# A hybrid decoder step on one core: B by token through VectorE and DRAM, state products in pairs, dt's sums in one visit

## The chip, the cores and the metric

The program runs on one of the eight NeuronCores of a Trainium2 chip. The metric is the device time of one execution in microseconds. The kernel before takes 1775.49 us in the median of three runs (1774.15 to 1775.97). The execution that was profiled took 1774.69 us, and its profile spans 1773.0 us.

The engines are called TensorE (PE in the profile; its weight loads PEld), VectorE (DVE), ScalarE (ACT), GpSimd (POOL) and SyncE (SP). SP computes nothing; it issues most DMA transfers. A line number L12 is a line of the kernel before.

## The reference, cut to what matters

The step takes 256 new tokens of one prompt and 8 sequences of 8 sample tokens, 320 tokens in all, through one layer. One input projection gives the columns of a gated MLP (u and v) and of a state-space mixer (z, x, B, C, dt). Both results go through an output projection; then a convolutional feed-forward network follows. All is in float32.

The change lies in the state-space mixer. Its state-space part is, cut down:

```python
dt = softplus(dt_raw + dt_bias);  a = -exp(a_log)
da_cs = cumsum(dt * a)                             # within a chunk of 128 tokens
decay = exp(mask(da_cs[t] - da_cs[s]))
cb = einsum("bctgn,bcsgn->bctsg", cc, bc)          # C times B, over the state
y_diag = einsum("bctsgr,bcsgrp->bctgrp", cb * decay, x * dt)
decay_states = exp(da_cs[last] - da_cs)
states = einsum("bcsgn,bcsgr,bcsgrp->bcgrpn", bc, decay_states, x * dt)
y_off = einsum("bctgn,bcgrpn,bctgr->bctgrp", cc, states_in, exp(da_cs))
```

There are 32 heads of 64 in 4 groups; each group has its own B and C with a state of 128. The prompt has two chunks of 128 tokens and starts from a zero state. The sample sequences are one short chunk each and start from given states (8 sequences x 4 groups x 128 x 512 numbers), which are also updated and returned.

## The kernel before, in words

**Tokens and features.** Activations are kept with features on the partitions and the 320 tokens along the row. Each weight product is split in three: weights and activations are each a rounded float32r part and a remainder (hi and lo), and `accumulate` (L153 to L155) multiplies hi by hi, hi by lo and lo by hi. A weight slab of 512 KB is loaded by SP, rounded by ScalarE (`whi`, L124), and its remainder is formed by VectorE (`wlo`, L125). Three slabs are in the buffers at a time. One slab is 8 blocks, so 24 products of TensorE.

**Order of work.** `project` runs an input projection over slabs. `chunk_out` adds four feature blocks of a finished part into the output projection. All other work is written as generators in the list `bg`. `tick` advances the first of them by one step; `project` and `chunk_out` call it after each slab, `rate` times. In `project` the last `quiet` of the 16 feature blocks have no ticks. `finish` advances until a given generator is done. The framework's planner then lays out a fixed order for each engine from priorities and its own model of times; work under `first()` or a high priority is drawn forward, so an operation can stand elsewhere than where it was written. On the chip each engine takes its own order strictly.

**The gate stage.** B and C are projected by `conv_proj` into `bT` and `cT` (features by tokens), then x of group 0. `steps` makes dt. It projects dt to tokens (L500), takes the softplus on VectorE, and after five empty steps goes to TensorE on three ticks: `cs_ps` (L532, L534) for the running sums by token, `csT_ps` (L547, L548) for the same sums by head, stored to DRAM as `dacs_d` and `tot_d`, and `dec_ps` (L560 to L567) for the decays to the end of a chunk; for the last one GpSimd makes a mask, `later_s`, just ahead of the products. Then `gate_mix` works out the MLP's gates by group (`sg`, L752).

**The state-space stage.** When the gate stage's buffers (pool `gp`) are free, pool `sd` takes their room. B is needed by tokens: 16 transposes by TensorE (`by_token` L414, into `bt_ps`), eight of them on rows of sample tokens that `fourfold` has copied four times, since four partition quarters of 32 rows need the same 32 tokens. ScalarE copies the results to `btok` and `bsp` (L802, L805), and VectorE forms remainders in two quarters of `bsp` (L807).

`ssd(g)` is a generator for each group. Its eight sample states are handled as four pairs. For a pair, `with_c` (L908) multiplies the states by C into `yo_ps` in eight TensorE instructions that each use 32 of the 128 columns of the array; `picked` (L913) makes the pair's B, `shrunk` (L919) decays the state on GpSimd, `grown` (L925, L927) multiplies B by x into `up_ps` and adds it to the state, and `store_state` writes it out. `begin` is with_c, picked and shrunk; `end` is grown and the store. Three pairs of state buffers are there, so pair 3 is loaded into those of pair 0 after its store. `x_of_samples` makes `xsp`, the samples' x that `grown` reads. Then `decays` and `products` make y (`y_ps`, L1004).

The groups' tasks run beside `heads_in_next` (x of the next group), `chunk_out` and `heads_out` (z, the norm, and the last product).

The loop of the pairs is:

```python
for i in range(4):
    if i < 3:
        begin(i)
    else:
        sts.append(load_state(3))
    if i:
        end(i - 1)
    yield
    if i == 0:
        x_of_samples(1)
    yield
begin(3)
yo_to_xdt()
```

Of the kernel before, what the change touches and what calls it, by code (L numbers as in the profile page):

```python
# [13 lines left out]
ALU = mybir.AluOpType  # L14
# [20 lines left out]
def hybrid_step(  # L35
# [325 lines left out]
    tot_d = dr.tile([NH, NB], F32, name="tot_d")  # L361
    ssq_d = [dr.tile([P, NT // 32], F32, name=f"ssq_d{i}") for i in range(4)]
# [52 lines left out]

    def fourfold(out, x, i):

        act.copy(out.rearrange("p k (q t) -> p k q t", q=4), x[:, :, NP + 32 * i:NP + 32 * i + 32].unsqueeze(2).to_broadcast([P, 4, 4, 32]))
        return out

    with ExitStack() as mctx:
# [6 lines left out]
        def conv_proj(c0, k0, out, *room):  # L428
# [27 lines left out]
            project(w_in, c0, evac, quiet=6)  # L456

        def heads_in(g, *room):
            xs = op.tile([P, 4, NT], F32, tag="xs", name="xs", bufs=2)
            conv_proj(X0 + 512 * g, 4 * g, lambda j: xs[:, j, :], *room)  # L460
# [27 lines left out]
        def steps():  # L488
# [26 lines left out]
            for n in (13, 11, 9, 7, 5, 3, 1):  # L515
# [9 lines left out]
                                     op0=ALU.mult, op1=ALU.mult)  # L525
            for _ in range(5):
                yield

            pool.memset(sums[:, 2], -3e38)
            ps = misc("cs_ps")  # L530
            for c in range(2):
                pe.matmul(ps[:, NH * c:NH * c + NH], upper, da[:, c], start=True, stop=True)  # L532
            for r in range(2):
                pe.matmul(ps[64 * r:64 * r + 64, 2 * NH:3 * NH], upper_s[:NS], da[:NS, 2], start=True, stop=True, tile_position=(0, 64 * r))  # L534
            dve.tensor_copy(sums[:, 0:2].rearrange("p c h -> p (c h)"), ps[:, :2 * NH])
# [9 lines left out]
            ps = misc("csT_ps")  # L545
            for c in range(2):
                pe.matmul(ps[:NH, P * c:P * c + P], da[:, c], upper, start=True, stop=True)  # L547
            pe.matmul(ps[:NH, NP:NT], da[:NS, 2], upper_s[:NS], start=True, stop=True)  # L548
            dacsT = op.tile([P, NT + NS + 2 * P], F32, tag="dtf", name="dacsT", bufs=1)[:, :NT + NS]
            dve.tensor_copy(dacsT[:NH, NS:], ps[:NH, :NT])  # L550
            dve.tensor_copy(dacsT[:NH, :NS], ps[:NH, NP:NT])
            sp.dma_start(dacs_d, dacsT[:NH])
            totc = op.tile([NH, NB], F32, name="totc")
            dve.tensor_copy(totc, dacsT[:NH, :NS].rearrange("p (b t) -> p b t", b=NB)[:, :, TS - 1])
            sp.dma_start(tot_d, totc)
            yield

            ps = misc("dec_ps")
# [877 lines left out]
```

## Time and profile before

| what | value |
|---|---|
| median of three runs | 1775.49 us (1774.15 to 1775.97) |
| the profiled execution | 1774.69 us, span 1773.0 us |
| TensorE busy | 1765.1 us (100%) |
| VectorE busy | 1173.7 us (66%) |
| ScalarE busy | 817.9 us (46%) |
| GpSimd busy | 274.5 us (15%) |
| mean granted clock | 0.999 |
| moved | 273.17 MB read, 14.84 MB written, 162 GB/s |

The profile is one execution. Its page gives busy time by engine, the span in 40 slices, the DMA queues, the chain of work that ended last, and the costliest groups of instructions. A busy TensorE isn't a TensorE at its best: its products are pipelined, and a product that started late still counts as busy. So the starts of its products, in the chain and in the timeline, say more than its share.

In the chain of waits a row gives start, length, engine, what was written, the line, and how many instructions are taken together. In a list of groups a row ends with the busy time, the mean length in ns, and the idle time of the engine ahead of it. A group with one line can be cut by tile.

### The profile page before, as it was taken

What the parts mean: (1) busy time and instruction counts of PE and PEld (TensorE: products, weight loads), DVE (VectorE), ACT (ScalarE), POOL (GpSimd) and SP (SyncE); (2) the same over time, 40 slices, a digit from 0 to 9 for tenths busy, and PEclk for the clock granted to TensorE, in tenths of its full rate; (3) what the DMA queues carried; (4) which work ended last, traced back from release to release, by engine and by line L of the source; (5) the groups of instructions that cost most, each with busy time, mean ns of one, the idle gap of its engine ahead of it and who ended that gap; (6) DMA issues with size and microseconds to landing.
All of it is one profiled execution on the core that took longest, in us unless ns stands there. A gap on an engine that the chain in (4) does not pass through costs nothing.

```text
span 1773.0 us, 30633 instructions
## 1 busy us (share of the span) xinstructions
PE 1765.1 (100%) x11897; PEld 1711.9 (97%) x11897; DVE 1173.7 (66%) x2015; ACT 817.9 (46%) x1193; POOL 274.5 (15%) x602
## 2 busy tenths in 40 slices
PE   9999999999999999999999999999999999999998
PEld 7789999999999998999999999999999999999998
DVE  7549764657978778678865465656657575656575
ACT  5434555334564556445645334343434343333445
POOL 1202200000331313103211011010102010101004
PEclk9999999999999999999999999999999999999999
DMA  7556645455666666555554554555455544454542
GB/s 261 161 150 171 189 141 159 153 152 182 223 189 195 186 203 188 147 179 158 171 158 147 154 153 148 155 148 153 150 151 158 144 156 145 156 155 145 155 151 102
DMA packets 217297, 290.01 MB, mean 164 GB/s; under 512 B 19264, under 2 KB 146624, under 8 KB 216960
## 3 DMA queue, kind: packets, MB, share of 16 engines
q1 hardware_dynamic: 205424, 268.84, 50.1%
q10 hardware_dynamic: 10016, 14.16, 2.2%
q0 software_dynamic: 1712, 5.05, 1.0%
q8 instruction: 94, 1.54, 0.4%
q14 instruction: 51, 0.42, 0.1%
HBM read 273.17 MB, written 14.84 MB: 162 GB/s over the span
## 4 chain that ended last, share of the span: by engine, by line
PE 98%; DVE 1%; issue 0%; ACT 0%; ACTq 0%; DVEq 0%
PE ps L153 19%; PE ps L154 19%; PE ps L155 19%; PE pd L153 10%; PE pd L155 10%; PE pd L154 10%; PE ps_v L144 7%; PE y_ps L1004 1%; PE up_ps L925 0%; PE sg L752 0%; PE yo_ps L908 0%; PE xt_ps L414 0%; PE early L70 0%; PE x1p L1299 0%; DVE xsp L863 0%
## 5 line engine op out<-in xcount | busy, mean ns | idle before, releaser
L125 DVE TENSOR_TENSOR wlo<-wraw,whi 128x1024 fp32r<-128x1024 f32 (+1 forms) x476 | 582.3, 1223 | 421.4 <-ACT whi L124 419.6
L124 ACT CAST whi<-wraw 128x1024 fp32r<-128x1024 f32 (+1 forms) x475 | 495.1, 1042 | 714.5 <-PE ps L154 381.5
L153 PE MATMUL ps<-h_hi,whi 128*128 128x320 f32 x2268 | 700.6, 309 | 0.0
L154 PE MATMUL ps<-h_lo,whi 128*128 128x320 f32 x2268 | 699.3, 308 | 0.0
L155 PE MATMUL ps<-h_hi,wlo 128*128 128x320 f32 x2268 | 698.9, 309 | 0.0
L153 PEld LDWEIGHTS ps<-h_hi,whi 128*128 128x128 f32 x2268 | 425.7, 188 | 2.5 <-issue 1.6
L154 PEld LDWEIGHTS ps<-h_lo,whi 128*128 128x128 f32 x2268 | 425.8, 188 | 0.7
L155 PEld LDWEIGHTS ps<-h_hi,wlo 128*128 128x128 f32 x2268 | 425.6, 188 | 0.0
L155 PE MATMUL pd<-fhi,wlo 128*128 128x320 f32 x704 | 217.0, 308 | 0.0
L153 PE MATMUL pd<-fhi,whi 128*128 128x320 f32 x704 | 217.0, 308 | 0.0
L154 PE MATMUL pd<-flo,whi 128*128 128x320 f32 x704 | 217.0, 308 | 0.0
L153 PE MATMUL pd<-ohi,whi 128*128 128x320 f32 x448 | 139.1, 310 | 0.0
L155 PE MATMUL pd<-ohi,wlo 128*128 128x320 f32 x448 | 138.4, 309 | 0.0
L154 PE MATMUL pd<-olo,whi 128*128 128x320 f32 x448 | 138.1, 308 | 0.0
L153 PEld LDWEIGHTS pd<-fhi,whi 128*128 128x128 f32 x704 | 132.2, 188 | 0.0
L154 PEld LDWEIGHTS pd<-flo,whi 128*128 128x128 f32 x704 | 132.2, 188 | 0.0
L155 PEld LDWEIGHTS pd<-fhi,wlo 128*128 128x128 f32 x704 | 132.2, 188 | 0.0
L1201 POOL COPY ptf<-pad 128x2 f32<-128x2 f32 x88 | 21.0, 238 | 602.7 <-DVE pad L1189 601.9
L249 DVE TENSOR_TENSOR acc_ffn<-acc_ffn,pd 128x320 f32<-128x320 f32 (+1 forms) x161 | 77.5, 482 | 37.8 <-PE pd L155 36.3
L153 PEld LDWEIGHTS pd<-ohi,whi 128*128 128x128 f32 x448 | 84.1, 188 | 1.6 <-issue 1.0
L154 PEld LDWEIGHTS pd<-olo,whi 128*128 128x128 f32 x448 | 84.1, 188 | 0.3
L155 PEld LDWEIGHTS pd<-ohi,wlo 128*128 128x128 f32 x448 | 84.1, 188 | 0.2 <-issue 0.2
(335 smaller groups left out, 1866.5 us busy)
## 6 DMA issues: line engine op xcount, KB each, us to landing
wraw<-in_ffn_w_up SPq DMA_DIRECT2D x176, 512.0 KB, 3.6
wraw<-in_w_in SPq DMA_DIRECT2D x140, 512.0 KB, 3.8
wraw<-in_ffn_w_down SPq DMA_DIRECT2D x88, 512.0 KB, 3.3
wraw<-in_w_out SPq DMA_DIRECT2D x64, 512.0 KB, 3.4
st<-in_state_ssm SPq DMA_DIRECT2D x32, 256.0 KB, 4.1
out_ssm_state_sample<-st ACTq DMA_DIRECT2D x30, 256.0 KB, 4.1
cs<-dacs_d SPq DMA_DIRECT2D x16, 320.0 KB, 4.7
xr<-in_xT SPq DMA_DIRECT2D x4, 640.0 KB, 4.0
```

The lines of the kernel that those rows point to most:

```text
L124: rounded[:] = [act.copy(hi, raw).ins]
L125: dve.tensor_tensor(out=lo, in0=raw, in1=hi.bitcast(F32), op=ALU.subtract)
L144: made = pe.matmul(out, xi, w[g][wi], start=first and begins, stop=last and ends)
L153: pe.matmul(ps, whi, xhi, start=first, stop=False)
L154: pe.matmul(ps, whi, xlo, start=False, stop=False)
L155: return pe.matmul(ps, wlo, xhi, start=False, stop=last).ins
L249: added_last[:] = [dve.tensor_tensor(out=acc[:, nb, ts], in0=acc[:, nb, ts], in1=ps[:, ts], op=ALU.add).ins]
L1004: pe.matmul(ps[64 * i:64 * i + 64, cols], w(hl), x(hl, m, cpx), tile_position=(0, 64 * i), **flags)
L1201: pool.tensor_copy(ptf[:, k, :], pad[:, 256:258])
```

## The change

- **B by token.** `to_tokens` takes `bT` 64 tokens at a time: VectorE transposes blocks of 32x32, and GpSimd's queue stores four pieces of 32 partitions to `b_d` in DRAM, five turns in all. The generator runs behind `steps`, and what is left of it is run after the first `gate_up`. Two loads on GpSimd's queue fetch the prompt's rows into `b_raw`, in the room of x. In the state-space stage two loads on SP's queue fetch the 32 sample rows four times each, into buffers `cs` that the decays use later. ScalarE copies them in the right order to `btok` and `bsp`; the remainders are formed as before. The 16 transposes of TensorE and the two fourfold copies of B are gone.
- **Pairs.** `with_c` of pairs 0 and 1 is written in one step, and of pairs 2 and 3 in one step six ticks after the update of pair 0. `picked`, `shrunk`, `end` and the second `x_of_samples` get places of their own; the updates of pairs 2 and 3 go into the steps of `decays`. A group's task takes one step more than before (two more in group 3).
- **Ticks.** In `heads_in_next` of groups 2 and 3 two ticks come with each slab.
- **dt.** The products of `cs_ps`, `dec_ps` and `csT_ps` are written in one step; the mask `later_s` and the memset of the sums' third part are made five steps ahead, in room that the decays' tile gives.

```diff
+    def to_tokens(x, rows):
+        for o in range(0, NT, NS):
+            t = tp.tile([P, NT], F32, tag="pv", name="turned", bufs=4)[:, :4 * NS].rearrange("p (r f) -> p r f", r=2)
+            dve.transpose(out=t.rearrange("p r (j f) -> p r j f", j=4), in_=x[:, :, o:o + NS].rearrange("p j (r t) -> p r j t", t=32))
+            for i in range(4):
+                pool.dma_start(rows[o:o + NS, P * i:P * i + P].rearrange("(r t) f -> t r f", t=32), t[32 * i:32 * i + 32])
+            yield
...
-            project(w_in, c0, evac, quiet=6)
+            project(w_in, c0, evac, quiet=6, rate=rate)
...
+            sums_of = op.tile([P, NT + NS + 2 * P], F32, tag="dtf", name="sums_of", bufs=1)
+            dacsT = sums_of[:, :NT + NS]
+            later_s = sums_of[:NS, NT + NS:].rearrange("p (r q t) -> p r q t", r=2, q=4)
+            for r in range(2):
+                rs = slice(32 * r, 32 * r + 32)
+                pool.tensor_tensor(out=later_s[:, r], in0=later[:NS, rs].unsqueeze(1).to_broadcast([NS, 4, 32]),
+                                   in1=bd[:, rs].unsqueeze(1).to_broadcast([NS, 4, 32]), op=ALU.mult)
+            pool.memset(sums[:, 2], -3e38)
             for _ in range(5):
                 yield
 
-            pool.memset(sums[:, 2], -3e38)
             ps = misc("cs_ps")
             for c in range(2):
                 pe.matmul(ps[:, NH * c:NH * c + NH], upper, da[:, c], start=True, stop=True)
+            ps_dec = misc("dec_ps")
+            for c in range(2):
+                pe.matmul(ps_dec[:, NH * c:NH * c + NH], later, da[:, c], start=True, stop=True)
+            pe.matmul(ps_dec[:, 2 * NH:3 * NH], ones, da[:, 1], start=True, stop=True)
+            for r in range(2):
+                pe.matmul(ps_dec[:, (3 + r) * NH:(4 + r) * NH], later_s[:, r].rearrange("p q t -> p (q t)"), da[:NS, 2],
+                          start=True, stop=True)
+            ps_T = misc("csT_ps")
+            for c in range(2):
+                pe.matmul(ps_T[:NH, P * c:P * c + P], da[:, c], upper, start=True, stop=True)
+            pe.matmul(ps_T[:NH, NP:NT], da[:NS, 2], upper_s[:NS], start=True, stop=True)
             for r in range(2):
                 pe.matmul(ps[64 * r:64 * r + 64, 2 * NH:3 * NH], upper_s[:NS], da[:NS, 2], start=True, stop=True, tile_position=(0, 64 * r))
+            dve.tensor_copy(dacsT[:NH, NS:], ps_T[:NH, :NT])
+            dve.tensor_copy(dacsT[:NH, :NS], ps_T[:NH, NP:NT])
+            sp.dma_start(dacs_d, dacsT[:NH])
...
             bg.append(tasks)
+            b_turned = to_tokens(bT, b_d)
+            bg.append(b_turned)
+            b_raw = op.tile([P, 4, NT], F32, tag="xs", name="b_raw", bufs=2).rearrange("p j n -> p (j n)")
             x0 = heads_in(0, rooms[0])
             finish(normed)
             uf = gate_up(0)
+            finish(b_turned)
+            for c in range(2):
+                pool.dma_start(b_raw[:, 512 * c:512 * c + 512], b_d[P * c:P * c + P])
...
             for c in range(4):
-                ps = misc("bt_ps")
-                b4 = bT if c < 2 else fourfold(sd.tile([P, 4, P], F32, tag="xde", name="b4", bufs=2), bT, c - 2)
-                for g in range(4):
-                    by_token(ps[:, P * g:P * g + P], b4[:, g], c if c < 2 else 0)
                 if c < 2:
-                    act.copy(btok[:, c, :], ps)
+                    raw, b = b_raw[:, 512 * c:512 * c + 512], btok[:, c]
                 else:
-                    b = bsp[:, c - 2]
-                    act.copy(b, ps)
-                    for rs in (slice(32, 64), slice(96, P)):
-                        dve.tensor_tensor(out=b[rs], in0=ps[rs], in1=b[rs].bitcast(F32), op=ALU.subtract)
+                    raw, b = sd.tile([P, 2, NT], F32, tag="cs", name="b4", bufs=3).rearrange("p i n -> p (i n)")[:, :512], bsp[:, c - 2]
+                    o = NP + 32 * (c - 2)
+                    sp.dma_start(raw, b_d[o:o + 32].unsqueeze(0).broadcast_to([4, 32, 512]))
+                act.copy(b.rearrange("p (j i f) -> p j i f", j=4, f=32), in_order(raw))
...
-                for i in range(4):
...
-                begin(3)
+                for i in range(2):
+                    bms[i] = picked(i)
+                yield
+                x_of_samples(1)
+                yield
+                for i in range(2):
+                    with_c(i, sts[i])
+                shrunk(0, sts[0])
+                yield
+                yield
+                end(0)
+                bms[2] = picked(2)
+                shrunk(1, sts[1])
+                yield
+                yield
+                end(1)
+                bms[3] = picked(3)
+                sts.append(load_state(3))
+                yield
+                yield
+                yield
+                yield
+                for i in range(2, 4):
+                    with_c(i, sts[i])
                 yo_to_xdt()
-                yield
-                if g < 3:
-                    end(3)
-                    yield
+                shrunk(2, sts[2])
+                yield
...
+                        if (j, i) == (0, 1):
+                            end(2)
+                            shrunk(3, sts[3])
+                        if (j, i) == (2, 1) and g < 3:
+                            end(3)
                         yield
...
             def heads_in_next(g):
-                x_of[g] = heads_in(g)
+                x_of[g] = heads_in(g, rate=2 if g > 1 else 1)
                 bg.append(tasks[g])
```

53 lines of the change are left out of this document (13 added, 40 removed).

## The prediction

> **What bounds the kernel now.** I read the head of the page and its chain of waits first, then the waits, then busy time by stretches.
>
> ```profile
> span 1773.0 us, 30633 instructions
> PE 1765.1 (100%) x11897; PEld 1711.9 (97%) x11897; DVE 1173.7 (66%) x2015; ACT 817.9 (46%) x1193; POOL 274.5 (15%) x602
> ...
> PE 98%; DVE 1%; issue 0%; ACT 0%; ACTq 0%; DVEq 0%
> ```
> ```profile
> ACT whi L124 <- PE ps L154: 381.5, 183, 4.3
> ```
> ```profile
> 180.00:260.00 80.00, 80.00 (x552) 78.99 (x551) 54.04 (x105) 43.36 (x64) 10.38 (x32) 1.00 0.54 159
> 420.00:760.00 340.00, 339.39 (x2481) 319.28 (x2480) 267.08 (x462) 191.53 (x354) 83.71 (x102) 1.00 0.62 192
> ```
> The reader should see that TensorE is never out of work: it is busy for 1765 of 1773 us and makes 98% of the chain. The row of the waits says that ScalarE waits for TensorE to give weight buffers back (381.5 us in all, up to 4.3 at a time), so the feeding engines run ahead by their buffers, and a hitch of VectorE or ScalarE shorter than about 4 us costs nothing. The stretches (columns: TensorE, weight loads, VectorE, ScalarE, GpSimd busy, clock, DMA share, GB/s) are those the change touches. VectorE is busy for 68% of the first and 79% of the second; there is room, but not much in the second. So the time moves only by what TensorE issues, and by gaps between its products. I therefore price every visit of small products that interrupts the weight stream.
>
> **The three visits of dt.** The chain of waits, start and length:
>
> ```profile
> 234.91 0.15 PE ps L155
> 235.05 0.36 PE cs_ps L532 x4
> 235.42 0.23 PE cs_ps L534 x4
> 235.65 0.34 PE ps L153
> ...
> 239.37 0.55 PE csT_ps L547 x4
> 239.93 0.23 PE csT_ps L548 x2
> 240.15 0.34 PE ps L153
> ...
> 243.87 0.36 PE dec_ps L560 x4
> 244.24 0.22 PE dec_ps L561 x2
> 244.46 0.23 PE ps L153
> 244.69 0.39 PE dec_ps L567 x2
> 245.07 0.34 PE ps L154
> 245.41 0.34 PE dec_ps L567 x2
> 245.75 0.34 PE ps L155
> ```
> A stream product takes 0.15; the first one behind a visit that used a part of the array takes 0.34, so the way back costs 0.19. Before: cs 0.36 + 0.23 + 0.19 = 0.78; csT 0.55 + 0.23 + 0.19 = 0.97; dec 0.36 + 0.22 + 0.08 + 0.39 + 0.19 + 0.34 + 0.19 = 1.77 (its last four products went out in pairs with stream products between). Together 3.52. After, in one visit: ten full-array instructions, 0.36 for the first four and 0.11 each for six (from the 0.22 for two), 1.02; later_s 0.39 for the first pair and, with no change of shape before the second, 0.27 (two at a quarter of csT's 0.55); csT 0.55 and 0.23; the masked sums 0.23; one way back 0.19. Sum 2.88, a gain of 0.64. Bounds: nothing, if the planner splits the visit as it split dec, and 1.0, if two of the changes of shape inside it cost nothing either (0.19 each).
>
> TensorEngine Tiling (Array Packing), Key Properties, in the Trainium skill says that a change of tiling mode, not of tile, drains TensorE. By it one counts changes of shape: nine before, five after, four saved; at the 0.19 of the rows that would be an estimated 0.76 for 0.64. The rows agree with the drain (0.34 for 0.15); the sum goes by the rows.
>
> What else this moves: the mask product of GpSimd and its memset go ahead of the visit, off TensorE's way; the stores of dacs_d and tot_d go out on SP's queue some 5 us earlier; their readers are far behind. VectorE's two copies now come before the copy of the sums; nothing is queued on that but exponentials of small tiles. Cost nothing, covered by the 32% of VectorE that is free.
>
> **B to tokens.** TensorE loses 16 transposes:
>
> ```profile
> 425.62 0.44 PE bt_ps L414 x4
> ...
> 426.50 0.44 PE bt_ps L414 x4
> ...
> 432.65 1.12 PE bt_ps L414 x8
> ```
> 2.00 us. A transpose uses the whole array, so there is no way back to gain. On ScalarE the four copies out of PSUM become four permuted copies out of SBUF, and two copies that made fourfold rows go; VectorE's four subtractions stay. Added: five block transposes of 128x256 on VectorE, 20 stores and two loads on GpSimd's queue, two broadcast loads on SP's. The nearest rows:
>
> ```profile
> L312 DVE STREAM_TRANSPOSE turned<-ssq 128x320 f32<-128x320 f32 x4 | 2.0, 510 | 0.1
> ```
> ```profile
> L736 POOL DMA_DIRECT2D wT<-in_gate_wT x4: 536/566/578, 84.5 to 380.5; - x4
> ```
> ```profile
> fst<-in_fconv SPq DMA_DIRECT2D x22, 32.0 KB, 2.9
> st<-in_state_ssm SPq DMA_DIRECT2D x32, 256.0 KB, 4.1
> ```
> Transposes: 5 x 0.51 x 256/320 = 2.0 us on VectorE, 2.6 at most by the full row, while it idles for 26 of the 80 us from 180 to 260. Stores and loads: 22 x 0.566 = 12.5 us of GpSimd, which is busy for 10.4 of those 80. A 32 KB store lands in about 2.9 us, a 256 KB load in 4.1, and the first reader of B by token stands at about 430, at least 150 us later. On GpSimd's queue the next groups' gate weights may stand behind them, but these wait for a spent buffer anyway. SP's two loads of fourfold rows stand ahead of the first state loads and, like them, wait for room that the gate stage frees; weight loads behind them can be late by some 3 to 4 us, against a stream that is three buffers ahead. I take nothing for all of it; the bounds are 0 and 12.5 (GpSimd's issue time, were it all in the way).
>
> **Two pairs' states in one visit.** Group 0's last visit, by the timeline of TensorE (start, length, line; the second row is the visit's first four instructions, asked for alone):
>
> ```profile
> 473.25 0.31 PE L155 MATMUL pd<-ohi,wlo 128*128 128x320 f32 x1
> 473.48 0.42 PE L908 MATMUL yo_ps<-st,cb_cms 128*32 128x256 f32 x4
> ...
> 473.48 0.64 PE L908 MATMUL yo_ps<-st,cb_cms 128*32 128x256 f32 x8
> 474.05 0.42 PE L153 MATMUL pd<-ohi,whi 128*128 128x320 f32 x1
> 474.31 0.32 PE L154 MATMUL pd<-olo,whi 128*128 128x320 f32 x1
> ```
> From the start of the stream product before to the start of the second one behind are 1.06 us, of which two stream products are 0.29: the visit costs 0.77. Each four instructions stream for 0.22 (0.64 less 0.42), so 0.44 is work and 0.33 the way in and out. Sixteen visits become eight, so 8 x 0.33 = 2.64 us go. Bounds: 0, if the planner lays stream products between the two pairs (as it did in dec); 2.64, as the work cannot go. I take 2.64: the states of pairs 0 to 2 are asked for at a group's first tick, as before, and used later than now.
>
> The update products move to later ticks. In group 1 they wait for xsp:
>
> ```profile
> 518.75 0.31 PE L155 MATMUL ps<-h_hi,wlo 128*128 128x320 f32 x1
> 519.30 0.47 PE L925 MATMUL up_ps<-xsp,bm 128*128 128x512 f32 x1 [0.24 <-DVE xsp L863]
> ```
> 0.55 between two starts for 0.15 is 0.40 lost, and group 3 has the same place in its chain. After the change the samples' second half is made two ticks and one visit ahead of its first use, so both losses should go: 0.80. Bounds: 0 and 0.80. What is late next is the state of pair 3 (below).
>
> The visits of y vary and are taken as they are; group 1's two:
>
> ```profile
> 576.38 1.69 PE y_ps L1004 x32
> ...
> 585.31 2.28 PE y_ps L1004 x31
> ```
> The 0.59 between them shows what one late operand costs. It can go or come in each of four groups: -2.4 to +2.4, taken as 0. The doubled rate of ticks in two projections makes two ticks fall on one slab; work is moved earlier by some 10 us into a stretch where VectorE has 21% free.
>
> **Sum.** 0.64 + 2.00 + 2.64 + 0.80 = 6.1 us. The profiled run took 1774.69, with a span of 1773.0, and should go to 1768.6; the median of the runs, 1775.49, stands 0.8 above it and should go to 1769.4, -0.34%. A measurement of this kernel tells about 0.2% (3.55 us) from no change.
>
> **Rivals.**
> *The merged visits don't stay whole and the waits stay.* Only the transposes and dt's sums count: 2.64, so 1772.9, within 0.2%. For it: dec's four visits in the rows above. Against: nothing there but a mask made too late split them.
>
> *Pair 3's state comes late* (slower). Its buffers are pair 0's: update, store, load. Now:
>
> ```profile
> 450.09 0.66 PE up_ps L925 x2
> ...
> 454.62 1.22 SPq L830 DMA_DIRECT2D st<-in_state_ssm  x2
> ...
> DMA to landing us min/median/max: 2.0/4.1/7.0
> ```
> From the update to both halves landed: 4.5 + 1.2 + 4.1 = 9.8 us. After, C's products with pair 3 come six ticks behind the update; at two ticks a slab of 24 stream products (24 x 0.15) that is 3 x 3.6 = 10.8 us, so 1 us is left. Were store and load each at the longest of the row, 2.9 more apiece, it would be 4.8 late in each of four groups, 19 us: 1775.5 - 6.1 + 19 = 1788.4. It decides from (6.1 + 3.55)/4 = 2.4 us a group. Against: the planner may place the visit later, and the load row's median leaves it in time.
>
> *B's way through DRAM stands in the way* (slower). Each convolution's evacuation needs a GpSimd memset; if four store issues (2.3 us) stand ahead of it in each of five turns, TensorE waits for a bank up to 11.3 us: 1775.5 - 4.1 + 11.3 = 1782.7. Against: the 70 us in which GpSimd has nothing to do.
> VectorE: DVE Perf Modes, Rules for kernel authors, in the Trainium skill gives a 128x128 transpose to TensorE where PSUM will do as the destination. By that rule the change would be a loss; the trace as it stands does not bear it out, since TensorE is the engine without room.
>
> *The y visits fall well* (faster still): 1769.4 - 2.4 = 1767.0.
>
> **How the numbers follow.** Forecast 0.72, y visits well 0.04: faster 0.76. Visits not whole: same 0.10. Late state 0.10, B in the way 0.04: slower 0.14. The point is 1769.4. The range runs from the lower case with a little noise, 1766.8, over the case without merging to 1775.0; above it lie the slower cases and a few hundredths of the same.
>
> **What would show it.** The chain of waits without bt_ps; one dt visit of about 2.9 us; eight visits of yo_ps x16, each 0.33 shorter than two; no wait of up_ps for xsp. It would be wrong if TensorE's starts show gaps of over 1 us at yo_ps waiting for st, if GpSimd's stores push pad memsets late near 190 to 220, or if VectorE, given two ticks a slab, delays wlo.

## The result and the profile after

The changed kernel takes 1778.71 us in the median of 11 runs (1777.05 to 1780.69); the kernel before took 1774.81 in 11 runs beside it (1773.47 to 1776.52). The ratio is 1.0022, with an interval of 1.0014 to 1.0030: about 3.9 us slower, where 6.1 us faster was forecast. The profiled execution spans 1777.9 us, 4.9 more than before.

The head of the page of the changed kernel and the end of its chain of waits:

```profile
span 1777.9 us, 30627 instructions
PE 1763.2 (99%) x11881; PEld 1713.5 (96%) x11881; DVE 1179.1 (66%) x2020; ACT 820.8 (46%) x1195; POOL 287.3 (16%) x624
...
PE 94%; DVE 3%; DMA 1%; ACT 1%; issue 1%; SPq 0%; ACTq 0%; DVEq 0%
```

TensorE works 1.9 us less and the kernel is longer: TensorE now stands still. In the stretch of the state-space stage that the prediction quoted it was busy for 339.39 of 340 us. The same columns for the changed kernel (span, then busy time of TensorE, weight loads, VectorE, ScalarE, GpSimd, then clock, DMA share, GB/s):

```profile
436.00:440.00 4.00, 3.32 (x14) 3.35 (x15) 1.37 (x2) 0.73 (x3) 0.00 (x0) 0.57 1.06 253
...
420.00:760.00 340.00, 332.50 (x2428) 314.94 (x2427) 265.71 (x451) 191.44 (x349) 84.91 (x102) 0.99 0.62 190
180.00:260.00 80.00, 80.00 (x558) 79.59 (x557) 56.46 (x112) 43.88 (x64) 22.77 (x54) 1.00 0.58 171
```

TensorE idles for 7.50 us of the 340 where it idled for 0.61, so 6.9 us were lost there. Nothing was lost from 180 to 260, where GpSimd's busy time doubled with the stores of B. The first row is a stretch at a mean granted clock of 0.57.

**What came in.** dt's visit, in the chain of the changed kernel (start, length, line):

```profile
235.40 0.36 PE cs_ps L553 x4
...
238.00 0.35 PE ps L153
```

From 235.40 to 238.00, with 0.20 for the way back, it costs 2.80, against 3.52 for the three visits before. A merged visit of the states times C, in the timeline of TensorE:

```profile
450.39 0.31 PE L155 MATMUL ps<-h_hi,wlo 128*128 128x320 f32 x1
450.63 1.07 PE L929 MATMUL yo_ps<-st,cb_cms 128*32 128x256 f32 x16
...
451.89 0.32 PE L154 MATMUL ps<-h_lo,whi 128*128 128x320 f32 x1
```

From the product before to the second one behind are 1.50 us, less two products (0.29): 1.21 for two pairs, where two visits cost 1.54. So 0.33 is saved, and by the starts of the products around the other visits, the same in five more of the eight and 0.26 in a seventh. The eighth, of pairs 2 and 3 in group 2, takes 1.80 us from 621.58 instead of 1.07, 0.27 more than two visits took before, because the weights of its products wait for the load of a state. The row of the weight loads' waits:

```profile
PEld yo_ps L929 <- DMA st<-in_state_ssm: 0.6, 1, 0.6
```

The transposes into `bt_ps` are gone, and TensorE waits no more at `up_ps` for xsp.

**What was lost in group 0.** The chain of the changed kernel:

```profile
433.74 2.94 issue
436.68 1.09 PE xt_ps L415 x4
437.77 0.27 PE ps L153
...
440.14 0.15 PE ps L153
...
446.75 0.43 PE xt_ps L415 x4
```

TensorE waits 2.94 us for the samples' x, then four transposes take 1.09 (0.43 later in the group) and nine stream products 0.27 instead of 0.15. That is 2.94 + 0.66 + (2.37 - 9 x 0.147 = 1.05) = 4.65 us. The cause is in the timeline of ScalarE; SP's queue stands behind it:

```profile
428.38 1.05 ACT L124 CAST whi<-wraw 128x1024 fp32r<-128x1024 f32 x1 [1.91 <-PE ps L154]
...
435.44 0.62 ACT L825 CAST bsp<-b 128x512 fp32r<-128x512 f32 x1 [4.26 <-DMA b<-b_d]
435.97 0.61 ACT L432 COPY x<-xs 128x512 f32<-128x512 f32 x1
439.85 0.62 ACT L825 CAST bsp<-b 128x512 fp32r<-128x512 f32 x1 [3.27 <-DMA b<-b_d]
440.38 1.05 ACT L124 CAST whi<-wraw 128x1024 fp32r<-128x1024 f32 x1
```
```profile
429.03 1.24 SPq L824 DMA_DIRECT2D b<-b_d  x2
```

The brackets hold the idle time before an instruction and what ended it. ScalarE waits 4.26 us for the first load of four-fold rows and 3.27 for the second. Between the two stands the copy of x that TensorE needs, and from 428.38 to 440.38 no weights are rounded. In the kernel before, the same copies waited 0.23 us, for TensorE, and x's copy stood behind them too:

```profile
433.30 1.10 ACT L805 CAST bsp<-bt_ps 128x512 fp32r<-128x512 f32 x2 [0.23 <-PE bt_ps L414]
...
437.65 0.60 ACT L418 COPY x<-xs 128x512 f32<-128x512 f32 x1
```

The two loads are issued at 429.03 and 429.76 and land at 435.42 and 439.83, so 6.4 and 10.1 us later; the median of the state loads, also 256 KB each, is 4.5 in this profile. The trace also has the signals by which a load reports its landing. A load of weights or of a state has sixteen of them, and each of these two ends with four. Of the weights' load issued next, at 430.71, twelve signals come by 436.19 and the last four from 440.71 to 441.07. This looks as if the four-fold loads ran on four of the sixteen DMA engines, one behind the other, and held back what followed there. A load with its four copies arranged in another way was not run.

**What was lost in group 1.** First the timeline of TensorE, then that of ScalarE, then SP's queue, all of the changed kernel:

```profile
514.16 0.66 PE L415 MATMUL xt_ps<-ident,x 128*128 128x128 f32 x4 [0.85 <-ACT x L432]
...
519.75 0.66 PE L415 MATMUL xt_ps<-ident,x 128*128 128x128 f32 x4 [1.27 <-ACT x L432]
```
```profile
507.50 0.40 ACT L1016 ACTIVATE cs<-cs,sums 128x128 f32<-128x128 f32 x1 [4.78 <-DMA cs<-dacs_d]
```
```profile
499.44 0.96 SPq L851 DMA_DIRECT2D st<-in_state_ssm  x2
...
500.96 0.42 SPq L858 DMA_DIRECT2D cs<-dacs_d  x1
```

ScalarE waits 4.78 us for a head pair's sums for group 1, with the copies of group 1's x behind it in its order, and TensorE waits twice for x. The load goes into one of three buffers that the second visit of y in group 0 gives back. It is issued at 500.96, behind two state loads that stood at the head of SP's queue until the stores of these states had ended, and it lands 6.4 us later, at 507.4. In the kernel before it is issued at 498.77, lands 4.2 us later, and ScalarE waits 2.53 us in the same place, though the profile names a product of TensorE as what ended the wait:

```profile
498.77 1.16 SPq L837 DMA_DIRECT2D cs<-dacs_d  x2
```
```profile
503.12 0.42 ACT L983 ACTIVATE cpx<-cs 128x256 f32<-128x256 f32 x1 [2.53 <-PE ps L154]
```

Before, the two y visits stood further apart and both were whole; the chains of before and of after:

```profile
485.36 1.69 PE y_ps L1004 x32
497.81 1.69 PE y_ps L1004 x32
```
```profile
489.71 1.69 PE y_ps L1030 x32
499.10 0.94 PE y_ps L1030 x16
```

They are 9.4 us apart instead of 12.4. A group's task has one step more; at two ticks a slab this puts the two visits two slabs apart, not three. The second visit is split: its other part starts at 502.75. The load that ScalarE waits for had gone out by then, so the split did not delay it. TensorE's other waits over the whole changed kernel (total, times, longest):

```profile
PE y_ps L1030 <- DVE cs L1019: 2.3, 3, 1.4
PE xt_ps L415 <- ACT x L432: 2.1, 2, 1.3
```

**The balance.** Gains of 0.72 + 2.0 + 2.0 (the merges: 6 x 0.33 + 0.26 - 0.27) = 4.7 us. Losses: 6.9 us idle (the two waits for xsp that went are already taken off in it), 1.7 at the low clock, and 0.8 in visits of y that are split, 9.4 together. A whole visit of y costs 1.9 us by the starts of the products around it, one in two parts 2.5 without its idle time; the kernel before had its split visits as well, and 0.8 is the difference over all four groups. The balance is 4.7 us longer; the span grew by 4.9.

### The profile page after: what moved, and what is told of

The parts are those of the page before. It is cut to its first block, busy times and chain, and to the rows that moved or that the text cites. A ratio compares the mean times of both kernels' runs of the same rounds, so it can differ in the third digit from the quotient of the medians.

```text
span 1777.9 us, 30627 instructions
## 1 busy us (share of the span) xinstructions
PE 1763.2 (99%) x11881; PEld 1713.5 (96%) x11881; DVE 1179.1 (66%) x2020; ACT 820.8 (46%) x1195; POOL 287.3 (16%) x624
## 3 DMA queue, kind: packets, MB, share of 16 engines
q8 instruction: 94, 1.54, 0.3%
## 4 chain that ended last, share of the span: by engine, by line
PE 94%; DVE 3%; DMA 1%; ACT 1%; issue 1%; SPq 0%; ACTq 0%; DVEq 0%
PE ps L153 18%; PE ps L155 18%; PE ps L154 18%; PE pd L153 10%; PE pd L154 10%; PE pd L155 10%; PE ps_v L144 7%; DVE wlo L125 1%; PE y_ps L1030 1%; PE sg L768 0%; PE xt_ps L415 0%; PE yo_ps L929 0%; DMA cs<-dacs_d 0%; DMA st<-in_state_ssm 0%; PE up_ps L946 0%
```

## The experiments

Each time is a median of 5 to 11 runs, with runs of the kernel before on the same chip. Ratios are to those, with 95% intervals; a thousandth is 1.8 us. A ratio is taken over all the runs, so it can differ from the quotient of the two medians by up to 0.6 thousandths, as much as 1 us. Traces show one run each. In the expectations, theory A is: the four-fold rows land late, ScalarE waits, x is late. Theory C is: two ticks a slab are too dense. Theory D is: the new order of pairs itself costs.

### The parts alone

dt's visit alone (the hunks from the tile `sums_of` to the stores, nothing else):

> The kernel before with dt's sums in one visit alone. All theories alike: TensorE gives back about 0.7 us (three visits of 3.6 us in all become one of 2.8), nothing else moves; 0.7 us faster than before, too little to be told from no change by the times, but to be seen in the starts of TensorE's products.

1773.75 us, ratio 0.9989 (0.9980 to 0.9998): 2.0 us faster by the ratio, 1.3 by the medians, with the predicted 0.64 inside the interval.

B's way through DRAM alone (`to_tokens`, `b_raw`, the two loads on SP's queue, the copies):

> The kernel before with B to tokens by VectorE and DRAM alone. Theory A (ScalarE's copy of the fourfold rows waits for their load from DRAM and holds the samples' x behind it, so TensorE waits some 3.2 us in group 0 and then runs at half clock for 2.5 us): the 16 transposes give 2.0 us, the wait takes 4.5 to 5, so 2.5 to 3 us slower than before. Theories C (two ticks a slab are too dense) and D (the new order of the pairs): no wait here, 2.0 us faster.

1779.23 us, ratio 1.0021 (1.0012 to 1.0029). ScalarE's waits and TensorE's wait at the same place:

```profile
ACT bsp L823 <- DMA b<-b_d: 7.8, 2, 4.4
```
```profile
437.45 0.66 PE L415 MATMUL xt_ps<-ident,x 128*128 128x128 f32 x4 [3.02 <-ACT x L432]
```

So the loss of group 0 comes from B's part and needs neither pairs nor ticks. Here the profile names ScalarE's copy of x as the releaser, which in the changed kernel it gave as "issue".

The pairs with the doubled rate, and the pairs at one tick a slab (`rate=2` left out):

> The kernel before with the pairs' new order and the doubled ticks of groups 2 and 3, B by TensorE's transposes and dt as before. Theory A (the waits in groups 1 and 2 follow from the late start of group 0): 3.4 us faster than before, by 2.6 for the merged visits and 0.8 for the two waits of the update products. Theories C and D (the waits at the samples' x in group 1 and at y in groups 0 to 2 come from the density or the order itself, 5 to 7 us in all): 2 to 4 us slower than before.

> The pairs' new order alone, one tick a slab in every input projection of x. Theory A: 3.4 us faster than before. Theory C (density): also 3.4 us faster, with no wait at y in groups 1 and 2 and no more table loads of ScalarE than before. Theory D (order): the waits stay, so no faster than before and up to 3 us slower.

1779.04 us, ratio 1.0021 (1.0012 to 1.0029), and 1781.73 us, ratio 1.0038 (1.0025 to 1.0050). Theory C falls: the doubled rate doesn't cost, and by the ratios it helps by some 3 us, though the two intervals overlap a little. The merged visits are whole in both; a row of TensorE's waits in the second:

```profile
PE xt_ps L414 <- ACT x L418: 5.0, 4, 1.3
```

The parts sum to -2.0 + 3.7 + 3.7 = 5.4 us, and the whole change is 3.9 slower. Each part is known to some 1.6 us only, so these runs can't tell whether the parts add.

### Four-fold rows: three tries to mend them

B alone, with the copies of the four-fold rows written behind group 0's x:

```diff
-                act.copy(b..., in_order(raw))          # rows c > 1, ahead of ssd(0)
+                fours.append((raw, b))
...
                 x_of_samples(0)
+                while fours:
+                    ordered(*fours.pop(0))
```

> The kernel before with B's new way alone, but the four-fold rows are brought into order by ScalarE behind its copy of group 0's x, not ahead of it. Theory A (the late load of these rows holds ScalarE, and with it x and TensorE): the pause of 3.3 us and the slow products behind it in group 0 (some 5 us together) go, and so most of the 4.2 us that B's new way alone lost: between 1 us slower and 2 us faster than the kernel before (2.0 us of transposes are saved). Rival (the loss lies elsewhere, such as later state loads behind the two new ones on SP's queue): it stays 3 to 5 us slower, or a new pause at the first products of C with the states takes the place of the old one.

1784.56 us, ratio 1.0046 (1.0034 to 1.0058). This tested nothing of theory A, because the planner laid the first copy ahead of x all the same, as the timeline of ScalarE shows; a longer wait of TensorE for xsp came on top later in the group:

```profile
436.62 0.62 ACT L819 CAST bsp<-b 128x512 fp32r<-128x512 f32 x1 [4.78 <-DMA b<-b_d]
437.14 0.61 ACT L432 COPY x<-xs 128x512 f32<-128x512 f32 x1
```

The changed kernel with GpSimd for the rows:

```diff
-                act.copy(b..., in_order(raw))
+                (act.copy if c < 2 else pool.tensor_copy)(b..., in_order(raw))
...
-                    dve.tensor_tensor(out=h, in0=in_order(raw[rs]), ...)
+                    pool.tensor_tensor(out=h, in0=in_order(raw[rs]), ...)
```

> The changed kernel, but the four-fold rows of B are brought into order and their remainders formed by GpSimd, so neither ScalarE nor VectorE has the late loads in its queue; the order of TensorE and of SP's queue is as in the changed kernel. In the run before this, the copies written behind group 0's x were still laid ahead of it by the planner, so that run says nothing of theory A. Theory A (ScalarE waits 4.3 us for the first of the loads, ahead of x's copy): group 0's pause of 3.25 us and the half clock behind it go, and the rest stays: 4 to 5 us faster than the changed kernel, so between 1 us faster and the same as the kernel before. Rival 1 (x or the products of C need something else that is as late): the pause stays at 2 us or more, or comes back at the first product of bm with xsp. Rival 2 (what is saved here is lost in the later groups): group 0's pause goes, but the time stays within 1.5 us of the changed kernel.

1779.91 us, ratio 1.0026 (1.0016 to 1.0036), so not faster than the changed kernel. The wait at the first x went and came back at the second. The timelines of ScalarE and of TensorE:

```profile
430.88 0.62 ACT L432 COPY x<-xs 128x512 f32<-128x512 f32 x1
...
443.90 0.91 ACT L934 ACTIVATE bm<-bsp,bsel 128x256 fp32r<-128x256 f32 x2 [8.47 <-POOL bsp L828]
444.71 0.60 ACT L432 COPY x<-xs 128x512 f32<-128x512 f32 x1
```
```profile
445.36 1.12 PE L415 MATMUL xt_ps<-ident,x 128*128 128x128 f32 x4 [2.84 <-ACT x L432]
```

The first x is copied at 430.88 and costs nothing. But ScalarE's next instruction that needs the rows, the product `bm`, stands ahead of the second x, and waits 8.47 us. So whoever copies them, the rows are late for what stands behind. How much of the 8.47 us is the loads isn't shown by this run, because GpSimd is slower too: its four subtractions take 5.1 us, VectorE's took 2.7.

Then the rows were loaded early: on GpSimd's queue, behind the loads of the prompt's rows, into dt's tile, the rest of `b_raw` and a buffer of the convolution:

```diff
+            b4 = [op.tile(..., tag="dtf", name="b4", bufs=1)[:, :512], b_raw[:, 1024:],
+                  op.tile([P, LP], F32, tag="cv", name="b4_h", bufs=2)[:, :256]]
+            for t, o, f in ((b4[0], NP, 0), (b4[1], NP + 32, 0), (b4[2], NP + 32, 256)):
+                n = 512 if o == NP else 256
+                pool.dma_start(t, b_d[o:o + 32, f:f + n].unsqueeze(0).broadcast_to([4, 32, n]))
...
-                    sp.dma_start(raw, b_d[o:o + 32].unsqueeze(0).broadcast_to([4, 32, 512]))
```

All of the change with it, and B alone with it:

> The changed kernel, but the four-fold rows of B are loaded some 100 us earlier, by GpSimd's queue behind the loads of the prompt's rows, into room that is free by then (dt's tile, the rest of the prompt's buffer, one buffer of the convolution); ScalarE and VectorE work on them as in the changed kernel. Theory A2 (what costs is that the rows land late, whichever engine waits for them: with GpSimd's copies the pause only moved from the first copy of x to the second, behind the product bm that needs the rows): both pauses of group 0 go, 4 to 5 us faster than the changed kernel, near the kernel before or up to 1.5 us faster. Rival (state loads or something else in group 0 is as late): a pause of over 2 us stays in group 0, and the time stays within 1.5 us of the changed kernel.

> The kernel before with B's way through DRAM alone, with early rows. With late rows it was 4.2 us slower than the kernel before. Theory A2: the 16 transposes' 2.0 us come in, 1 to 2.5 us faster than the kernel before. Rival (B's way costs elsewhere): slower than the kernel before still.

1776.89 us, ratio 1.0003 (0.9994 to 1.0012), and 1775.29 us, ratio 0.9996 (0.9988 to 1.0005). Against the same kernels with late rows that is 3.4 us (1.0022 to 1.0003) and 4.4 us (1.0021 to 0.9996), each known to some 2 us. Group 0's pause is gone; a stretch of all of the change with early rows:

```profile
436.00:440.00 4.00, 4.00 (x26) 3.52 (x25) 3.93 (x10) 1.96 (x3) 0.00 (x0) 1.00 0.69 225
```

That the late rows cost group 0's 4 us is shown by this. B alone then gains 0.7 us by its ratio. The interval, from 2.1 us faster to 0.9 slower, just holds the 2.0 of the transposes, but the profile shows where some of it went. The timelines of VectorE and of TensorE in B alone:

```profile
494.17 1.23 DVE L125 TENSOR_TENSOR wlo<-wraw,whi 128x1024 fp32r<-128x1024 f32 x1 [4.51 <-ACT whi L124]
```
```profile
495.85 0.42 PE L153 MATMUL ps<-h_hi,whi 128*128 128x320 f32 x1 [1.44 <-DVE acc_mix L249]
```

TensorE, some 1.6 us ahead of the kernel before at 441, waits here for a PSUM bank. Its evacuation stands behind `wlo`, and `wlo` waits for ScalarE, which in this kernel waits up to 3.8 us for a decay's sums (at most 2.5 before). Time won in group 0 was given back one group later.

### The additional step

One of the four empty steps ahead of the products of C with pairs 2 and 3 is taken out:

```diff
                 sts.append(load_state(3))
                 yield
                 yield
                 yield
-                yield
                 for i in range(2, 4):
                     with_c(i, sts[i])
```

in the pairs alone at one tick a slab; in the changed kernel; with GpSimd's rows; with early rows; and in all of the change at one tick a slab with the copies that were meant to come late:

> The kernel before with the new order of pairs alone, one tick a slab, and one of the four empty steps ahead of the products of C with pairs 2 and 3 taken out, so that a group's task has as many steps as in the kernel before. Theory of the steps (one step more moves y's two visits nearer to each other or to the next group's x, so that the second comes late, is split, and frees the decays' buffers late): the pauses of TensorE behind it go; 2 to 4 us faster than the kernel before (2.6 for the merged visits, 0.8 for xsp). Rival (the order of pairs itself costs, whatever the count of steps): as slow as with four empty steps, 4 to 7 us slower than the kernel before; if pair 3's state is then too late, pauses at yo_ps show it.

> The changed kernel with one of the four empty steps taken out, nothing else. Theory of the steps: the pauses at x of group 1 (1.2 and 1.6 us), and those at y of groups 1 and 2 (1.8 and 0.9) go, while group 0's pause stays: 3 to 6 us faster than the changed kernel, so 2 us faster to 1 us slower than the kernel before. Rival (the order itself): no faster than the changed kernel.

> As the run with GpSimd's rows, and one of the four empty steps taken out. The empty step was worth 1.9 us against the changed kernel (2.7 at one tick a slab). Theory A and the theory of the steps as separate causes: they add, so 5.5 to 7 us faster than the changed kernel, 2 to 3 us faster than the kernel before. Rival (one cause: whichever is mended, the next late operand takes its place): no more than 1 us faster than with GpSimd's rows alone.

> As the run with early rows, and one of the four empty steps taken out (worth 1.9 us so far, with either place of the rows). If the two losses add: 6 to 7 us faster than the changed kernel, 2 to 3 us faster than the kernel before. If they overlap: no more than 1 us faster than with early rows alone.

> All of the change with both mends (the four-fold rows brought into order behind group 0's x; one empty step taken out) and one tick a slab. If theory A and the theory of the steps hold and together make up the loss: the sum of the terms that the trace showed to arrive (dt 0.75, transposes 2.0, merges 2.7, xsp 0.8), so 4 to 6 us faster than the kernel before. If only A holds: within 2 us of the kernel before. If neither: 3 us slower or more.

| kernel | ratio with the step | ratio without it |
|---|---|---|
| pairs alone, one tick | 1.0038 | 1.0026 (1.0017 to 1.0034) |
| the changed kernel | 1.0022 | 1.0007 (0.9998 to 1.0015) |
| with GpSimd's rows | 1.0026 | 1.0018 (1.0009 to 1.0026) |
| with early rows | 1.0003 | 1.0000 (0.9991 to 1.0009) |

Their times are 1780.16, 1776.89, 1778.18 and 1775.37 us. All four go the same way, by 0.5 to 2.7 us. In each pair the intervals overlap, so it is the four together that speak for the step, and no size is settled. In the changed kernel the waits at x of group 1 are gone and y's are smaller, 1.0 us for 2.3. The load of sums that ScalarE waits for is issued at 499.43 there, and the wait is 3.60 us for 4.78. A row of TensorE's waits without the step:

```profile
PE up_ps L946 <- DVE xsp L884: 0.9, 2, 0.5
```

The waits at xsp are back, so the 0.80 that the prediction counted is lost with the step. The order of the pairs alone stays slower than the kernel before with as many steps as that: the theory of the steps explains a part and not the whole. The fifth kernel took 1782.32 us, ratio 1.0037 (1.0023 to 1.0050). The planner laid its copies ahead of x as in B alone, so it was no mended version.

### x's copy taken out of ScalarE's order

Theory E is: in the later groups a decay of ScalarE that waits for its sums holds the copy of x. VectorE, and then GpSimd, copies x:

```diff
-        act.copy(out..., x[:, :, NP + 32 * i:...].to_broadcast([P, 4, 4, 32]))
+        dve.tensor_copy(out..., ...)       # in the last two: pool.tensor_copy
```

> As the run with GpSimd's rows, and VectorE instead of ScalarE copies the samples' x four-fold in all groups. Theory E (in the later groups too ScalarE's order is the cause: a decay that waits 4.8 us for its sums stands ahead of the copy of x): TensorE's waits at x in group 1 (1.2 and 1.6 us) go and nothing takes their place: 1 to 3 us faster than with GpSimd's rows alone. Rival (VectorE is full, and eight copies of some 0.5 us make wlo or y late): no faster than with GpSimd's rows alone, or slower, with new pauses at the weight stream or at y.

> All three: GpSimd's rows, VectorE's copy of x, one empty step less. If all three causes are separate: 7 to 9 us faster than the changed kernel, 3 to 5 us faster than the kernel before, near the sum that the prediction gave. If VectorE has no room: slower than with GpSimd's rows and the step alone.

> All of the change with early rows, and GpSimd's copy of x; one edit away from the run of all of the change with early rows. Theory E: TensorE's waits at x in group 1 (1.1 and 1.6 us) go: 1 to 2.5 us faster than that run. What is left then are y's waits (2.1 and 0.9 us), which GpSimd's copy does not touch. Rival: the pauses stay or move, no faster than that run.

1783.18 us (1.0049, 1.0037 to 1.0062), 1782.99 us (1.0045, 1.0032 to 1.0057) and 1779.65 us (1.0027, 1.0016 to 1.0038): 3 to 5 us slower than without the edit. TensorE still waits for x; the row of the waits with VectorE's copy (the first of the three) and with GpSimd's (the last):

```profile
PE xt_ps L415 <- DVE x L432: 6.5, 2, 4.1
```
```profile
PE xt_ps L415 <- POOL x L432: 4.6, 4, 3.0
```

With GpSimd the copy waits for `s_ps`, whose operand holds one of the two buffers that x's copy is written to (last row), and for xdt (first), ahead of it in GpSimd's order:

```profile
511.52 1.04 POOL L880 TENSOR_TENSOR xde<-xdt,dec 128x512 f32<-128x512 f32 x1 [6.15 <-DVE xdt L874]
...
516.14 0.62 POOL L432 COPY x<-xs 128x512 f32<-128x512 f32 x1 [3.02 <-PE s_ps L926]
```

Theory E falls as a mend: ScalarE's order held x in the changed kernel, but another engine's order and the buffers hold it as long.

### Towards a version that beats both

B with early rows and dt's visit, without pairs; and the same with GpSimd's copy of x:

> B's way with early rows and dt's sums in one visit, without the new order of pairs and without the doubled rate. If the pairs' order is what is left of the loss: 2 to 4 us faster than the kernel before (dt's visit alone was 1.3 us faster), and faster than all of the change with the mends. Rival (the two disturb each other, as the parts of the change did): no faster than dt's visit alone.

> B's way with early rows and dt in one visit, as in the run before, and GpSimd instead of ScalarE copies the samples' x four-fold, where no decay that waits for its sums stands ahead of it. That run had one pause left, 1.5 us at x in group 1. Theory E (ScalarE's order is the cause): it goes, 1 to 2 us faster than that run, 1.5 to 3.5 us faster than the kernel before. Rival (GpSimd's copy is slower, 1.2 us for 0.6, or its queue is held by something else): new waits at x, no faster than that run.

1774.75 us (0.9997, 0.9988 to 1.0005) and 1776.02 us (1.0003, 0.9994 to 1.0011). Neither tells from the kernel before. The one that does is dt's visit alone, at 0.9989, and its interval ends at 0.9998; it is also 3.3 thousandths below the changed kernel.

TensorE's idle time in the 340 us from 420 to 760 (340 less its busy time in each kernel's row of stretches) stands beside these ratios:

| kernel | idle, us | ratio |
|---|---|---|
| before | 0.61 | 1 |
| dt's visit alone | 2.10 | 0.9989 |
| B with early rows, dt | 2.42 | 0.9997 |
| B with early rows | 2.55 | 0.9996 |
| all, early rows, one step less | 4.94 | 1.0000 |
| all, early rows | 4.64 | 1.0003 |
| all, one step less | 5.96 | 1.0007 |
| B alone | 5.69 | 1.0021 |
| the change | 7.50 | 1.0022 |
| pairs, one tick | 7.31 | 1.0038 |
| B alone, copies meant late | 9.65 | 1.0046 |
| all, GpSimd's rows, VectorE's x | 10.13 | 1.0049 |

The eight kernels that are left out have 4.50 to 9.41 us. No kernel has less idle time than the kernel before. Idle time ranks the kernels only roughly (5.96 us at 1.0007, 5.69 at 1.0021), and a trace is one run: dt's visit alone touches nothing in this stretch and yet shows a wait of 1.4 us at y, in the slowest of its 11 runs.

## Why the prediction was wrong

**The terms of the gain were nearly right.** dt's visit: 0.64 forecast, 0.72 in the rows (2.80 against a forecast 2.88). Merges: 2.64 forecast, 2.0 in the rows; the planner kept all eight whole, but one waited for a state. The transposes: gone. The two waits for xsp: gone in the changed kernel, and they come back when a step is taken out. So TensorE was spared some 5.5 of the 6.1 us.

**The step that failed first** is the sentence on B's loads that ends "I take nothing for all of it". It weighed SP's two loads only for "weight loads behind them", and ScalarE's four copies only by their number. It didn't ask what the copies wait for, nor what stands behind them on ScalarE. The prediction had part of it in its own words: these loads wait for room that the gate stage frees, which came at 429 us, and its 4.1 us for a load puts the rows at 433 at the earliest. That "the first reader of B by token stands at about 430, at least 150 us later" holds for the prompt's rows alone. The 4.1 us was wrong here as well: the four-fold loads took 6.4 and 10.1. Before the change the operand came from TensorE and was waited for 0.23 us. After it the copies wait 4.26 and 3.27 us, the copy of x stands between them, and x has no three buffers of slack as the weights have. That is 4.65 us in the rows, and 3.4 and 4.4 us by the runs with early rows.

With it fell the sentence that "a hitch of VectorE or ScalarE shorter than about 4 us costs nothing". The 381.5 us that ScalarE waited for weight buffers are slack of the weight stream alone. An operand like x, asked for a few microseconds after it can first be made, has none.

**The step that failed second** is "The visits of y vary and are taken as they are", with -2.4 to +2.4 "taken as 0", and the additional step of a group's task, which was told and not priced. y's waits cost 2.3 us and those of group 1's x 2.1 us. Taking the step out gave 0.5 to 2.7 us. The way from the step to x is read from the traces and not tested link by link: y's two visits move together, the load of a head pair's sums goes out 2.2 us later and takes 2.2 us longer to land, a decay waits 4.78 us where it waited 2.53, and x waits behind it. The split visits of y, also not priced, cost 0.8.

**The rivals.** *Pair 3's state comes late* happened once, and small: the products with pairs 2 and 3 of group 2 wait 0.6 us for a state load, where the prediction's worst case had 4.8 in each group. Its median case left 1 us of room. *The merged visits don't stay whole* did not happen. *B's way through DRAM stands in the way* was the right part of the change with the wrong place: GpSimd's stores cost nothing (TensorE is busy for 80.00 of the 80 us from 180 to 260), and SP's loads, 190 us later, cost 4. Its chance of 0.04 was for that wrong place alone. The rule of VectorE: DVE Perf Modes, Rules for kernel authors, in the Trainium skill, which leaves 128x128 transposes to TensorE, spoke against the change; the runs bear it out in so far as the other way gained nothing that can be measured (0.9996, 0.9988 to 1.0005, at its best).

The doubled rate was left without a cost, and the runs show none: by the ratios it helps by some 3 us against the pairs at one tick.

**What stays open.** With early rows, about 0.5 us remain above the kernel before, where the sum says 6 below. The runs of all of the change with early rows fall in two bunches, 1775.0 to 1775.6 and 1776.9 to 1777.5, and the trace is of the lower; what parts them isn't known. The traces show that the gains are given back as waits at x, at y and at PSUM banks in groups 1 to 3, and that moving one copy to another engine only moves the wait. Why the order of pairs alone stays 4.6 us slower with as many steps as before is open too. Which order of steps would keep the gains wasn't found. A fourth buffer for the decays' sums, which would test that link of the chain by itself, wasn't tried: there was no room for it.

## What to carry to other kernels

When an operand's source moves from an engine to a load, ask of its first reader: how long before the reader's turn can the load be issued, and what stands behind the reader on its in-order engine. Idle shares don't answer that, and neither does the slack of the weight stream. Where TensorE is busy for 99.8% of a stretch, work taken from it is worth its length only if every operand behind it can come earlier by as much; check the next operand's releaser before counting the gain. A load's price should come from a load of the same shape, and not only of the same size: here 256 KB took 4.5 us in the median of the state loads, and 6.4 and 10.1 in the four-fold ones. And moving a late operand's consumer to another engine shows whether it is the engine or the operand that is late, if the other engine is as fast: here the wait moved along, and GpSimd's own time came on top.

## What the runs showed of the hardware

The clock falls to half after some pauses of TensorE of 2 to 3 us, but not after each. In the changed kernel a pause of 2.94 us was followed by a granted clock of 0.57 from 436 to 440. In all of the change with early rows and one step less, a wait of 1.87 us was enough; with GpSimd's copy of x, one of 2.99 us was not. The timeline of TensorE and the stretch behind it, of the one and then of the other:

```profile
494.70 0.42 PE L153 MATMUL ps<-h_hi,whi 128*128 128x320 f32 x1 [1.87 <-DVE acc_mix L249]
```
```profile
495.00:498.00 3.00, 3.00 (x16) 2.67 (x16) 2.08 (x4) 2.55 (x7) 0.00 (x0) 0.58 0.85 222
```
```profile
513.17 0.66 PE L415 MATMUL xt_ps<-ident,x 128*128 128x128 f32 x4 [2.99 <-POOL x L432]
```
```profile
513.00:517.00 4.00, 3.76 (x22) 3.02 (x23) 3.42 (x6) 2.05 (x3) 0.73 (x2) 1.00 0.23 82
```

So the price of a pause of this length isn't its length alone; in the changed kernel 1.7 us of slow work came on top of 2.94. The Trainium skill, TensorE: Matmul & The Clock Gate, What's actually happening, says that the gate looks at TensorE's activity in windows of about 3.4 us that run freely, and halves the clock after an idle one. That the same pause may count or not agrees with windows that run freely; that 1.87 us sufficed does not agree with a whole idle window being needed.

The traces say more. In their record of the clock each low stretch amid a kernel is at 0.50 and lasts 3.41 us, and the changes of one trace lie whole multiples of 3.41 us apart. Cut the time from 420 to 760 us on that grid, in all twenty traces. Each of the twelve stretches in which TensorE idles for 1.99 us or more is followed by a low one, none with 1.50 or less is, and of the five from 1.60 to 1.92 three are. The pause of 2.94 us lay almost whole in one stretch; that of 2.99 fell on two, 1.07 in the first and 1.92 in the second. So it counts where a pause lies, and about half of a stretch is enough; what decides between 1.60 and 1.92 stays open.
